# Outputs of three expert quads kept as DRAM rows and gathered in the fourth quad, in place of one-hot scatter products

## The chip, the cores and the metric

The kernel runs on one core of a Trainium2 chip. The metric is the device time of one execution in microseconds. The kernel before takes 929.15 us, the median of three runs (928.97 to 929.91).

## The reference, cut to what matters

Two trunk layers, each a mixer and then a mixture of 16 experts in 4 groups; a token goes to the best group and there to its best two experts. Layer 0 works on 512 tokens (256 latent, 256 context), layer 1 on the 256 latent ones. All in float32, width 1024, expert width 512.

```python
pg, g = lax.top_k(p_grp, 1)                       # group of the token
pe, ie = lax.top_k(jax.nn.softmax(logits_sel), 2)  # two experts in it
wts = pg * pe / jnp.sum(pe, axis=-1, keepdims=True)
eid = g * EXPERTS_PER_GROUP + ie
for e in range(N_EXPERTS):
    a = jax.nn.silu(h @ w_gate[e]) * (h @ w_up[e])
    y = y + gates[:, e:e + 1] * (a @ w_down[e])
x = x + g2 * y
```

So 1024 pairs (token, expert) in layer 0, each with one output row of 1024 numbers, and each token adds two such rows.

## The kernel before, in words

The change is in the experts of layer 0 (function `experts`, with `l == 0`). The 16 experts are taken in four "quads" of four. A quad has 384 slots, as three tiles of 128 (`nst = 3`): each expert has 64 slots in the first two tiles and 32 more in the third, and the third tile is worked on only in quads where some expert has more than 64 pairs. In the traced execution that is so in quads 1 and 2. Code that runs only then stands under `beyond(q)`, a branch on a register that every engine takes by itself.

A quad takes three phases of four weight chunks, 2 MB each: gate (`wg`, into PSUM banks `ga`), up (`wu`, into `ua`) and down (`wd`, into `da`). The down phase has two halves of 512 output columns, each of two chunks. Weights come by SyncE's DMA queue into a ring of five buffers and one more (`slot0`), so chunk n is fetched when TensorE has let go of chunk n - 6. PSUM has four `acc` banks, two `aux` and two `tmp`.

TensorE's input for a quad is `XT`, its tokens' rows, transposed. For quads 1 to 3, `slots(q)` builds a one-hot matrix `SS` (slot by token), `fetch` makes an index per slot out of it (`ii`, on VectorE, three buffers) and GpSimd gathers the rows from DRAM (`xg`, three buffers of 128 x 1024, an indirect DMA each; from quad 2 on a second one for the gates). `turn` transposes them, between the matmuls of the quad before.

What a quad puts out is added to the tokens by matmuls: `halves` splits a half of the output into two parts `oh` (ScalarE's cast) and `ol` (VectorE's difference), `combine` multiplies both by `SS` (128x512 matmuls, two for each 128 columns and tile), and `add` multiplies by the gate of the modulation and adds into `X` (`xl` latent, `xc` context, tokens along the free axis). The second half's `combine` of a quad is `pending` and runs behind the first gate chunk of the next quad. The last quad does the same with its last 512 columns cut in two.

The order on each engine is that of a list scheduler, except for instructions under `tc.keep_in_program_order`, which stay as written. Engines take their instructions in that order, so one that waits holds all behind it.

The code ahead of the experts that matters here: the routing (`Route.choose`, `Route.slots`, one chain on VectorE, shown under line 89, the wrapper that pins it) ends in `vec`, from which the `OH` one-hots (`one_hots`) of quad 0 are built; TensorE waits for these before it gathers quad 0's tokens by matmul (line 1036).

Of the kernel before, what the change touches and what calls it, by code (L numbers as in the profile page):

```python
# [12 lines left out]
F32 = mybir.dt.float32  # L13
# [22 lines left out]
HW = 0  # L36
EXTRA = 1
CAP = {0: 96, 1: 64}


PAR_BMOD, PAR_NG, PAR_WR, PAR_BR, PAR_PSC = 0, 96, 128, 448, 488
PAR_W = 492

CO_ID, CO_ONE, CO_TOK, CO_SLOT, CO_BEFORE, CO_BASE, CO_QUAD, CO_FIRST = 0, 128, 256, 768, 788, 804, 836, 840
CO_W = 844

MC_ROT, MC_MASK = 0, 512
MC_W = 768
# [8 lines left out]
def build(tc, ctx, a, cap=CAP):  # L57
# [7 lines left out]
    shd = dram.tile([1, 2 * D], F32, name="shd")  # L65
    h2d = dram.tile([T, D], F32, name="h2d")
    gd = dram.tile([T, 4], F32, name="gd")

    def phase(name, side="left"):
        return tc.tile_pool(name=name, bufs=1, side=side, reuse_waits="tile")  # L70
# [97 lines left out]


    def transpose(out, in_):  # L170
        PE.transpose(out, in_, ident)  # L171

    def keep_warm(n, bank=tmp):

# [141 lines left out]
    def drain(g):  # L316
        out = None
        for out in g:
            pass
        return out  # L320
# [433 lines left out]
    class Route:  # L754


        def __init__(self, l, nt, small, rt):
            self.l, self.nt, self.rt = l, nt, rt
            self.small, self.used = small.tile([P, 130 * nt], F32, name="small"), 0
            self.vec = small.tile([P, 4, nt], F32, name="vec")  # L760
            self.gov = small.tile([P, nt, 16], F32, name="gov")
            self.flag = small.tile([P, 1], I32, name="flag")
            self.plan = small.tile([P, 8], I32, name="plan")

        def new(self, *shape):
# [103 lines left out]
        def slots(self, rk):  # L869
            l, nt = self.l, self.nt  # L870
            V_ = pinned(V)
            r = rk[:, 0:nt * 16].rearrange("p (t c) -> p t c", t=nt)
            ov = self.ov = self.new(nt, 16)
            V_.tensor_scalar(ov, r, float(CAP[l]), None, op0=ALU.is_ge)
            t = self.rt.work[:, 0:48 * nt]
            t0 = t[:, 0:nt * 16].rearrange("p (t c) -> p t c", t=nt)
            V_.scalar_tensor_tensor(t0, ov, -1e6, self.base[:, None, :].to_broadcast([P, nt, 16]),
                                    op0=ALU.mult, op1=ALU.add)
            V_.tensor_tensor(t0, t0, r, op=ALU.add)
            m = t[:, nt * 16:nt * 48]  # L880
            V_.tensor_tensor(m.rearrange("p (i m) -> p i m", i=2), self.M.rearrange("p (i t) c -> p i (t c)", i=2),
                             t[:, None, 0:nt * 16].to_broadcast([P, 2, nt * 16]), op=ALU.mult)
            V_.tensor_reduce(self.vec[:, 0:2, :].rearrange("p i t -> p (i t)"),
                             m.rearrange("p (m c) -> p m c", c=16), axis=AX.X, op=ALU.add)

        def gates(self):
            nt, new, over = self.nt, self.new, self.over
# [156 lines left out]
                    V.tensor_scalar(XT[:, k, c0:c1], y[:, :W], sh[k], None, op0=ALU.add)  # L1044


    def experts(l, nt, h2, vec, gov, fv, place, more, XT, xpool, pool, where, last):
        n = nt * P
        nst = 3 if l == 0 else 2
        W = nst * P  # L1050
# [113 lines left out]
        if l == 0:  # L1164
            x8 = slot0[0].tile([P, 2048], F32, tag="x", name="x8")
            yg = itertools.cycle([x8[:, 1536:1792], x8[:, 1792:2048]])
        pending = []
        sq = []
        quad = [0]
        for q in range(4):  # L1170
# [4 lines left out]
            for ch in range(4):  # L1175
                w = ahead.pop(0) if ahead else weights(a["wg"][l, place[q], ch])
                drain(tiles([(ch * 2 + kk, XT[:, ch * 2 + kk, :], w[:, kk]) for kk in range(2)], KD - 1, ga,
                            ch % 2 == 0))
                if ch == 0:
                    while pending:  # L1180
                        pending.pop()()
                if ch == 1 and q == 2:
                    overflow(l, nt, h2, gov, fv, pool)
                if ch == 0 and q == 0:
                    rows(range(2))
                    if l == 0:
                        nSS, xg = slots(1)
                if ch == 1 and q == 0:
                    rows(range(2, 4))
                    SS, _ = slots(0, False)  # L1190
            sg = []
            for st in range(2):
                t = pool.tile([P, DE], F32, tag="sg", name="sg", bufs=3 - l)
# [5 lines left out]
            for ch in range(4):  # L1199
                w = weights(a["wu"][l, place[q], ch])  # L1200
                drain(tiles([(ch * 2 + kk, XT[:, ch * 2 + kk, :], w[:, kk]) for kk in range(2)], KD - 1, ua,
                            ch % 2 == 0))
            if l:
                gt = gates(q)
            elif q == 0:
                gts = gates(0), gates(1)
                gt = gts[0]
            turning = iter(())
            if q < 3:
                if l:  # L1210
# [11 lines left out]
            def turned(st):  # L1222
                tp = tmp()
                for f in range(4):
                    transpose(tp[:, f * P:(f + 1) * P], sg[st][:, f * P:(f + 1) * P])
                V.tensor_copy(aT[:, :, st * P:(st + 1) * P], tp.rearrange("p (f t) -> p f t", f=4))  # L1226

            for st in range(2):
                V.scalar_tensor_tensor(sg[st], ua[st], gt[:, st:st + 1], sg[st], op0=ALU.mult, op1=ALU.mult)  # L1229
                turned(st)  # L1230
            if nst == 3:
                sg.append(pool.tile([P, DE], F32, tag="sg", name="sg", bufs=3 - l))
                with beyond(q):
                    S.activation(sg[2], ga[2], AF.Silu)
                    V.scalar_tensor_tensor(sg[2], ua[2], gt[:, 2:3], sg[2], op0=ALU.mult, op1=ALU.mult)
# [12 lines left out]
            def halves(da, c0=0, c1=512, parts=None):  # L1248
                if parts is None:
                    parts = [pool.tile([P, nst, 512], F32R, tag=x, name=x, bufs=2 - l) for x in ("oh", "ol")]  # L1250

                def part(st):
                    oh, ol = [x[:, st, c0:c1] for x in parts]
                    S.copy(oh, da[st][:, c0:c1])  # L1254
                    V.tensor_tensor(ol, da[st][:, c0:c1], oh.bitcast(F32), op=ALU.subtract)  # L1255

                part(0)
                part(1)
                if nst == 3:
                    with beyond(q):  # L1260
                        part(2)
                return parts

            def combine(hf, parts, k0=0, k1=4, bank=acc, q=q, SS=SS):
                for kk in range(k0, k1, 2):
# [33 lines left out]
                    nc.scalar.dma_start(a["out"][:, k, :], X[0][:, k, :])  # L1299

            da = [[acc() if hf == 0 or i < nst - 2 else aux() for i in range(nst)] for hf in range(2)]
            if q < 3:
                p = []
                for hf in range(2):
                    for c in range(2):
# [43 lines left out]
    for l in range(L):  # L1349
# [21 lines left out]
        with phase(f"mix{l}", "right") as pool:  # L1371
# [40 lines left out]
            OH = one_hots(nt, W, names, ro.vec, keep, ("pT", "s512"), T, 4, F32 if l else F32R, pinned(V))  # L1412
            if l == 0:
                drain(ro.plans)
            next(filler, None)
            if l == 0:
                for tt in range(nt):
# [8 lines left out]
        with phase(f"xt{l}") as hp:  # L1426
# [23 lines left out]
            keep_stack.close()  # L1450
            with phase(f"ex{l}") as pool:
                where = itertools.cycle([ring] * 5 + ([spare] * EXTRA + early if l else slot0))
                nxt = experts(l, nt, None if l == 0 else h2, vec, gov, fv, place, more, XT, hp, pool, where, l == L - 1)
        rp_stack.close()
        slot_stack.close()

# [2 lines left out]
def constants():  # L1459
# [12 lines left out]
    co[:, CO_BASE + 16:CO_BASE + 32] = np.arange(16) * 64 + 1  # L1472
    co[:, CO_QUAD:CO_QUAD + 4] = np.arange(4)
    co[:, CO_FIRST:CO_FIRST + 4] = [-100, 1, 2, 3]

    mc = np.zeros((P, MC_W), f)
    mb = np.zeros((P, MB_PW), f)
# [101 lines left out]
```

## Time and profile before

| | |
|---|---|
| median of three runs | 929.15 us |
| the profiled execution | 929.26 us |
| its span, first to last instruction | 927.4 us |
| mean granted TensorE clock | 0.979 |
| TensorE busy (PE) | 865.7 us, 93% |
| VectorE (DVE), ScalarE (ACT), GpSimd (POOL) busy | 409.9, 265.9, 64.5 us |
| bytes moved by DMA | 287.14 MB, mean 310 GB/s |

The profiled execution is 1.86 us longer than its span, and 0.11 us above the median. In the rows, a timeline row gives start, length, engine, line, operation, output and input with their size, and in brackets the idle time of the engine ahead of it and what ended it. Layer 0's experts run from about 262 to 552 us: quad 0 to 326, quad 1 to 411, quad 2 to 495, and the last quad to 552; then comes layer 1.

### The profile page before, as it was taken

How to read it: one execution, taken by the hardware profiler on the slowest of the kernel's cores; microseconds unless marked ns; L12 is line 12 of the kernel's file. 1: busy time of each engine (PE TensorE's matmuls, PEld its weight loads, DVE VectorE, ACT ScalarE, POOL GpSimd, SP SyncE). 2: the span in 40 equal slices, each digit the busy share in tenths (PEclk: the TensorE clock that was granted, in tenths of full speed). 3: DMA queues.
4: the chain of work that ended last, by engine and by line, in shares of the span. 5: the costliest groups of instructions: out<-in, count | busy, mean ns of one | idle time of the engine just before them, and what ended most of it. 6: DMA issues, size and time to landing. Idle time of an engine off the chain costs nothing. (4 is left out here: it accounts for less than half of the span.)

```text
span 927.4 us, 13199 instructions
## 1 busy us (share of the span) xinstructions
PE 865.7 (93%) x5078; PEld 478.1 (52%) x5078; DVE 409.9 (44%) x1028; ACT 265.9 (29%) x579; POOL 64.5 (7%) x74
## 2 busy tenths in 40 slices
PE   3899999999589999999999989989999999979998
PEld 2588676776353332442344357756973444434435
DVE  1467677633975230332221148877555241222212
ACT  3344667424320100110011055466422011100101
POOL 1000000001410030012000020000000000000000
PEclk9999999999699999999999998999999999989999
DMA  9645753744979999759958953985978999999981
GB/s 359 277 177 207 290 214 137 281 182 160 357 269 429 426 370 423 306 211 363 426 211 334 382 216 117 412 357 199 366 304 313 430 424 428 428 410 427 428 288 47
DMA packets 33826, 287.14 MB, mean 310 GB/s; under 512 B 3533, under 2 KB 13389, under 8 KB 17105
## 3 DMA queue, kind: packets, MB, share of 16 engines
q1 hardware_dynamic: 29168, 276.94, 74.3%
q0 software_dynamic: 1696, 5.79, 1.6%
q10 hardware_dynamic: 2880, 3.35, 1.0%
q8 instruction: 49, 0.80, 0.3%
q14 instruction: 33, 0.26, 0.1%
HBM read 282.90 MB, written 3.16 MB: 308 GB/s over the span
## 5 line engine op out<-in xcount | busy, mean ns | idle before, releaser
L1136 PE MATMUL acc<-w,XT 128*64 128x512 f32 (+1 forms) x768 | 171.3, 604 | 9.1 <-PEq L950 5.5
L1136 PE MATMUL aux<-w,XT 128*64 128x512 f32 (+1 forms) x512 | 109.1, 593 | 0.7 <-PEq L1146 0.7
L1136 PEld LDWEIGHTS acc<-w,XT 128*64 128x64 f32 (+1 forms) x768 | 51.5, 134 | 108.0 <-issue 103.8
L1136 PEld LDWEIGHTS aux<-w,XT 128*64 128x64 f32 (+1 forms) x512 | 33.6, 130 | 66.1 <-issue 65.3
L1136 PE MATMUL acc<-w,x 128*64 128x512 f32 (+2 forms) x272 | 55.3, 575 | 2.9 <-PEq L1146 2.3
L192 PE MATMUL aux<-w,c 128*32 128x512 f32 x368 | 49.5, 657 | 0.0
L1229 DVE SCALAR_TENSOR_TENSOR sg<-aux,gt,sg 128x512 f32<-128x512 f32 x12 | 9.0, 750 | 82.1 <-PE aux L1136 81.4
L115 DVE TENSOR_TENSOR wl<-w,wh 128x768 fp32r<-128x768 f32 (+2 forms) x48 | 43.8, 955 | 3.1 <-ACT wh L115 2.7
L1255 DVE TENSOR_TENSOR ol<-acc,oh 128x512 fp32r<-128x512 f32 (+1 forms) x25 | 15.7, 627 | 57.2 <-ACT oh L1254 57.0
L137 PE MATMUL acc<-wh,hh 128*128 128x512 f32 x96 | 38.3, 399 | 2.2 <-ACT hh L300 2.2
L1254 ACT CAST oh<-acc 128x512 fp32r<-128x512 f32 (+1 forms) x25 | 13.4, 534 | 94.0 <-PE acc L1136 93.9
L115 ACT CAST wh<-w 128x768 fp32r<-128x768 f32 (+2 forms) x48 | 37.5, 831 | 7.9 <-DMA w<-w_out 3.8
L138 PE MATMUL acc<-wl,hh 128*128 128x512 f32 x96 | 37.9, 394 | 0.0
L139 PE MATMUL acc<-wh,hl 128*128 128x512 f32 x96 | 37.8, 393 | 0.0
L1194 ACT ACTIVATE sg<-acc 128x512 f32<-128x512 f32 x16 | 9.4, 597 | 87.0 <-PE acc L1136 87.0
L525 ACT ACTIVATE pr<-acc,soft 128x512 f32<-128x512 f32 (+1 forms) x48 | 29.4, 619 | 11.7 <-DVE soft L522 11.7
L1136 PEld LDWEIGHTS acc<-w,x 128*64 128x64 f32 (+1 forms) x272 | 15.6, 130 | 32.6 <-issue 31.6
L1136 PE MATMUL aux<-w,aT 128*64 128x512 f32 (+2 forms) x192 | 29.1, 453 | 0.0
L1136 PE MATMUL acc<-w,aT 128*64 128x512 f32 (+1 forms) x160 | 28.8, 511 | 0.2 <-DVE aT L1226 0.2
L574 PE MATMUL aux<-pT,vt 128*64 128x128 f32 x320 | 27.3, 281 | 0.4 <-ACT pT L549 0.2
L1102 ACT COPY XT<-tmp 128x512 f32<-128x512 f32 x6 | 3.5, 585 | 81.6 <-PE tmp L171 81.6
L1292 DVE SCALAR_TENSOR_TENSOR xl<-tmp,modT,xl 128x256 f32<-128x256 f32 x24 | 11.2, 481 | 33.2 <-PE tmp L1272 33.0
(329 smaller groups left out, 1581.7 us busy)
## 6 DMA issues: line engine op xcount, KB each, us to landing
w<-wg SPq DMA_DIRECT2D x32, 2048.0 KB, 13.1
w<-wu SPq DMA_DIRECT2D x32, 2048.0 KB, 11.5
w<-wd SPq DMA_DIRECT2D x29, 2048.0 KB, 12.0
w<-w_mod SPq DMA_DIRECT2D x23, 2048.0 KB, 12.6
w<-w_out SPq DMA_DIRECT2D x4, 2048.0 KB, 8.3
w<-wd SPq DMA_DIRECT2D x6, 1024.0 KB, 13.4
w<-w_qkv SPq DMA_DIRECT2D x3, 1536.0 KB, 8.3
w<-w_pf SPq DMA_DIRECT2D x2, 2048.0 KB, 7.9
```

The lines of the kernel that those rows point to most:

```text
L115: return S.copy(hi, x), eng.tensor_tensor(lo, x, hi.bitcast(F32), op=ALU.subtract)
L137: PE.matmul(out, lhs[0], rhs[0], start=start, stop=False, skip_group_check=True)
L138: PE.matmul(out, lhs[0], rhs[1], start=False, stop=False, skip_group_check=True)
L139: PE.matmul(out, lhs[1], rhs[0], start=False, stop=stop, skip_group_check=True)
L192: mm = PE.matmul(m[32 * j:32 * j + 32, :], sc2[:, k, :], w[:, kk, j * 512:(j + 1) * 512], start=(ch == chs[0] and kk == 0), stop=(ch == ch ...
L525: S.activation(pr[e], sp[e], AF.Exp, bias=nm[:, e:e + 1], scale=SCALE, accum_out=sums[:, e:e + 1])
L574: PE.matmul(o[e * 64:(e + 1) * 64, c * P:(c + 1) * P], vt[:, k0 + m, e * 64:(e + 1) * 64], pTs[e * nk + m], start=(m == 0), stop=(m == nk ...
L1136: PE.matmul(o, lh, r, start=(k == 0), stop=(k == last_k), skip_group_check=True)
L1194: S.activation(t, ga[st], AF.Silu)
L1254: S.copy(oh, da[st][:, c0:c1])
L1255: V.tensor_tensor(ol, da[st][:, c0:c1], oh.bitcast(F32), op=ALU.subtract)
L1292: V.scalar_tensor_tensor(x, y[:, s * N:(s + 1) * N], g, x, op0=ALU.mult, op1=ALU.add)
```

## The change

In layer 0 the outputs of the first three quads are no longer multiplied by `SS`. A new `store` copies each tile of a half from PSUM to SBUF (ScalarE the first and third tile, VectorE the second) and GpSimd's queue writes it, 128 rows of 512 numbers, to its place in a DRAM array `yd` of 1152 rows and one row of zeros. Without a third tile something else is written in its place. That is 18 writes of 256 KB.

A new `places`, nine operations on VectorE in the routing, makes for every token the two rows of `yd` that it adds (the row of zeros for a pair that isn't in the first three quads). `collect`, called after the third and the fourth chunk of the last quad's up phase, gathers these rows on GpSimd's queue, two indirect DMAs of 512 KB for each of four tiles of 128 tokens, adds the two on VectorE (pinned), transposes the sum on TensorE (32 transposes in all, pinned) and adds it into `X` with the modulation's gate. The last quad keeps its scatter products.

```diff
@@ class Route
+        def places(self, rk):
+            nt = self.nt
+            c16 = [co[:, CO_ROW + i * 16:CO_ROW + (i + 1) * 16] for i in range(2)]
+            r = rk[:, 0:nt * 16].rearrange("p (t c) -> p t c", t=nt)
...
+            V.tensor_tensor(b, self.base, c16[1], op=ALU.add)
+            V.tensor_scalar(t, r, 64.0, None, op0=ALU.is_ge)
+            V.tensor_tensor(t, t, c16[0][:, None, :].to_broadcast([P, nt, 16]), op=ALU.mult)
+            V.tensor_tensor(t, t, r, op=ALU.add)
+            V.scalar_tensor_tensor(t, self.ov, 1e6, t, op0=ALU.mult, op1=ALU.add)
+            V.tensor_tensor(t, t, b[:, None, :].to_broadcast([P, nt, 16]), op=ALU.add)
+            V.tensor_tensor(m.rearrange("p (i t) c -> p i (t c)", i=2), self.M.rearrange("p (i t) c -> p i (t c)", i=2),
+                            t.rearrange("p t c -> p (t c)")[:, None, :].to_broadcast([P, 2, nt * 16]), op=ALU.mult)
+            V.tensor_reduce(f, m, axis=AX.X, op=ALU.add)
+            V.tensor_scalar(self.rows, f, float(YD), None, op0=ALU.min)
@@ experts, ahead of the quads
+            z = pool.tile([P, D], F32, tag="xg", name="z", bufs=3)
+            G.memset(z[0:1, :], 0.0)
+            G.dma_start(yd[YD:YD + 1, :], z[0:1, :])
+        def collect(tts):
+            for tt in tts:
+                if tt in (1, 2):
+                    g = [pool.tile([P, nst, 512], F32, tag=("oh", "ol")[tt - 1], name="yr", bufs=2)[:, 0:2, :]
+                         .rearrange("p a b -> p (a b)") for _ in range(2)]
+                else:
+                    g = [pool.tile([P, D], F32, tag="xg", name="yr", bufs=3) for _ in range(2)]
+                for i in range(2):
+                    G.indirect_dma_start(out=g[i], out_offset=None, in_=yd[:, :],
+                                         in_offset=bass.IndirectOffsetOnAxis(ap=places[:, i * nt + tt:i * nt + tt + 1], axis=0))
+                tc.keep_in_program_order(V.tensor_tensor(g[0], g[0], g[1], op=ALU.add))
+                for i in range(2):
+                    t = tmp()
+                    for c in range(4):
+                        tc.keep_in_program_order(
+                            transpose(t[:, c * P:(c + 1) * P], g[0][:, (i * 4 + c) * P:(i * 4 + c + 1) * P]))
+                    for c in range(4):
+                        k = i * 4 + c
+                        x = X[tt // 2][:, k, tt % 2 * P:tt % 2 * P + P]
+                        V.scalar_tensor_tensor(x, t[:, c * P:(c + 1) * P], modT[l][:, 40 + k, tt // 2:tt // 2 + 1], x,
+                                               op0=ALU.mult, op1=ALU.add)
@@ experts, in a quad
-                    SS, _ = slots(0, False)
+                    SS = None if l == 0 else slots(0, False)[0]
...
+                if l == 0 and q == 3 and ch > 1:
+                    collect(range(2 * ch - 4, 2 * ch - 2))
...
-                gts = gates(0), gates(1)
-                gt = gts[0]
+                gt = gates(0)
...
+            def store(da, hf):
+                ys = pool.tile([P, nst, 512], F32, tag=("oh", "ol")[hf], name="ys", bufs=2)
+                def put(st, y):
+                    r0 = q * 384 + st * P
+                    G.dma_start(yd[r0:r0 + P, hf * 512:(hf + 1) * 512], y)
+                for st in range(2):
+                    (V.tensor_copy if st else S.copy)(ys[:, st, :], da[st])
+                    put(st, ys[:, st, :])
+                with beyond(q) as there:
+                    S.copy(ys[:, 2, :], da[2])
+                    put(2, ys[:, 2, :])
+                with there.Else():
+                    put(2, ys[:, 0, :])
...
-            if q < 3:
+            if l == 0 and q < 3:
+                for hf in range(2):
+                    for c in range(2):
+                        down(da[hf], 2 * c, weights(wd(l, place[q], 2 * hf + c)))
+                    store(da[hf], hf)
+            elif q < 3:
@@ layer 0, routing
                 drain(ro.plans)
+                ro.places(rk)
```

How this moves instructions is seen at three places. The first is TensorE in the last quad, from the last matmuls of the third up chunk to the transposes of `sg` ahead of the down phase; before:

```order
L1136 MATMUL aux<-w,XT 64x512 x2
L1146 COMPARE_AND_BRANCH
L1136 MATMUL aux<-w,XT 32x512 x16
L1146 UNCONDITIONAL_BRANCH x2
L1233 COMPARE_AND_BRANCH
L1233 UNCONDITIONAL_BRANCH x2
L1136 MATMUL acc<-w,XT 64x512 x2
L1136 MATMUL aux<-w,XT 64x512 x2
L1136 MATMUL acc<-w,XT 64x512 x2
L1136 MATMUL aux<-w,XT 64x512 x2
L171 MATMUL tmp<-co,sg 128x128 x8
```

and now, where `yr` is a gathered sum of rows, the end of the third chunk:

```order
L1161 MATMUL aux<-w,XT 64x512 x2
L173 MATMUL tmp<-co,yr 128x128 x8
L1171 COMPARE_AND_BRANCH
L1161 MATMUL aux<-w,XT 32x512 x16
L1171 UNCONDITIONAL_BRANCH x2
```

with, a few rows on, the fourth chunk:

```order
L1161 MATMUL acc<-w,XT 64x512 x2
L1161 MATMUL aux<-w,XT 64x512
L173 MATMUL tmp<-co,yr 128x128 x8
L1161 MATMUL aux<-w,XT 64x512
L1161 MATMUL acc<-w,XT 64x512 x2
L1161 MATMUL aux<-w,XT 64x512 x2
L173 MATMUL tmp<-co,yr 128x128 x16
L173 MATMUL tmp<-co,sg 128x128 x8
```

The eight transposes of the first token tile stand right behind the third chunk, those of the second inside the fourth chunk, and those of the third and fourth behind it, ahead of everything of the down phase.

The second place is GpSimd from quad 2's second half on (the stores of quad 2's first half stand just ahead of these rows); before, none of these DMAs stands there.

```order
L1324 DMA yd<-ys 128x512 [waits DMASW2_49,Activation_49]
L1329 UNCONDITIONAL_BRANCH
L1324 DMA yd<-ys 128x512 [waits DMASW3_49]
L1324 DMA yd<-ys 128x512 [waits DMASW4_49,DVE_49]
L1204 DMA yr<-yd,rows 128x1024 [waits DMASW3_49,DMASW4_49,DMASW2_49,DMASW5_49,DMASW1_49,DMASW7_49,DMASW0_49,PE_49]
L1204 DMA yr<-yd,rows 128x1024 [waits DMASW6_49,PE_49]
L1204 DMA yr<-yd,rows 128x1024 x2
L869 TENSOR_LOAD plan
L1171 COMPARE_AND_BRANCH
L1171 UNCONDITIONAL_BRANCH x2
L1204 DMA yr<-yd,rows 128x1024
L1204 DMA yr<-yd,rows 128x1024 [waits Activation_49]
```

The first gather waits for the landing of the stores (the DMASW semaphores are those of GpSimd's queue).

The third place is VectorE in quad 0's down phase, between its first and second half. Before, `ol` is the split of the output:

```order
L1104 COPY XT<-tmp 128x4x128 [waits PE_49]
L1146 COMPARE_AND_BRANCH
L1146 UNCONDITIONAL_BRANCH x2
L1260 COMPARE_AND_BRANCH
L1255 TENSOR_TENSOR ol<-acc,oh 128x512 [waits DVE_49,Activation_49]
L1260 UNCONDITIONAL_BRANCH
L1260 UNCONDITIONAL_BRANCH [waits DVE_49]
L1104 COPY XT<-tmp 128x4x128 [waits PE_49]
L1255 TENSOR_TENSOR ol<-acc,oh 128x512 [waits DVE_49,Activation_49]
L1104 COPY XT<-tmp 128x4x128 [waits PE_49]
```

and now, where `ii` is an index of the fetches for the last quad:

```order
L1129 COPY XT<-tmp 128x4x128 [waits PE_49]
L1329 COMPARE_AND_BRANCH
L1329 UNCONDITIONAL_BRANCH x2
L1109 TENSOR_SCALAR ii<-ix 128x1 [waits DMASW7_49,DMASW2_49]
L1327 COPY ys<-acc 128x512 [waits DMAHW2_49,PE_49]
L1107 SCALAR_TENSOR_TENSOR sk,ix<-SS,co 128x512 [waits DVE_49]
L1129 COPY XT<-tmp 128x4x128 [waits PE_49]
L1109 TENSOR_SCALAR ii<-ix 128x1 [waits DMASW5_49,DMASW0_49]
L1109 TENSOR_SCALAR ii<-ix 128x1 [waits DMASW7_49,DMASW1_49,DVE_49]
```

The scheduler has pulled the index work for the last quad up into quad 0. Each `ii` takes the buffer of one of quad 2's indices and waits for that fetch to land, and the copies of quad 0's output out of PSUM (`ys<-acc`, and a `ys<-aux` after these rows) stand behind it.

## Rows read from the trace of the kernel before

**Rows 1.** The page, busy time of TensorE.
```profile
PE 865.7 (93%) x5078; PEld 478.1 (52%) x5078; DVE 409.9 (44%) x1028; ACT 265.9 (29%) x579; POOL 64.5 (7%) x74
```
**Rows 2.** Busy time by stretch: the four quads (the last in two), then layer 1's start.
```profile
core 0: us, PE busy (x) PEld busy (x) DVE busy (x) ACT busy (x) POOL busy (x), PEclk, DMA share, GB/s
262.00:326.00 64.00, 60.37 (x280) 24.94 (x277) 33.50 (x87) 9.49 (x16) 4.67 (x5) 1.00 0.93 382
326.00:411.00 85.00, 83.37 (x477) 32.27 (x478) 23.23 (x50) 9.60 (x18) 11.03 (x13) 1.00 0.85 342
411.00:495.00 84.00, 81.79 (x472) 31.23 (x470) 22.25 (x47) 8.65 (x16) 9.35 (x11) 1.00 0.81 323
495.00:525.00 30.00, 29.02 (x132) 10.49 (x129) 2.28 (x5) 1.67 (x3) 0.73 (x1) 1.00 0.88 346
525.00:552.00 27.00, 24.53 (x136) 12.72 (x134) 9.13 (x19) 9.42 (x22) 5.24 (x6) 1.00 0.80 295
552.00:564.00 12.00, 9.04 (x42) 5.75 (x40) 8.53 (x18) 5.64 (x12) 1.43 (x2) 0.58 0.00 0
```
**Rows 3.** SyncE's queue, waits in quads: line, waited for, us, times, longest.
```profile
SPq L108 <- PE acc L1136: 109.1, 19, 11.6
```
**Rows 4.** The same view by stretch, 298 to 326 us alone.
```profile
298.00:326.00 28.00, 25.98 (x115) 10.79 (x113) 9.02 (x17) 4.46 (x8) 1.46 (x2) 1.00 1.01 427
```
**Rows 5.** Scatter products of quads 0 to 2 alone, line 1272, by eleven stretches.
```profile
314.00:318.70 4.70, 3.16 (x11) 1.84 (x11) 1.00 1.00 425
...
497.00:499.00 2.00, 0.96 (x3) 0.48 (x3) 1.00 0.04 16
sum 40.40, PE 33.89 PEld 22.70; mean PE 3.08 PEld 2.06
```
**Rows 6.** Timeline of TensorE: transposes of fetched rows, last quad's start, its down phase.
```profile
374.30 1.06 PE L171 MATMUL tmp<-co,xg 128*128 128x128 f32 x8 [0.83 <-PE tmp L171]
...
494.27 3.65 PE L1136 MATMUL acc<-w,XT 128*64 128x512 f32 x16
...
526.50 3.65 PE L1136 MATMUL acc<-w,x 128*64 128x512 f32 x16 [0.30 <-PEq L1244]
...
551.87 0.40 PE L1272 MATMUL acc<-SS,ol 128*128 128x512 f32 x1
```
**Rows 7.** Timeline of VectorE: the routing; quad 1's first tile leaves `xg`.
```profile
245.58 0.28 DVE L89 TENSOR_TENSOR rw<-small,rw 128x128 f32<-128x128 f32 x1
...
309.99 0.69 DVE L1104 COPY XT<-tmp 128x512 f32<-128x512 f32 x1
```
**Rows 8.** TensorE's waits, 240 to 262 us.
```profile
PE acc L1036 <- DVE OH L89: 5.9, 1, 5.9
```
**Rows 9.** GpSimd's fetches of rows, 334 to 450 us: issue to landing.
```profile
DMA to landing us min/median/max: 10.7/15.8/18.5
```
**Rows 10.** Timeline of ScalarE: third and last copies out of quad 2's output banks.
```profile
472.43 0.59 ACT L1254 CAST oh<-acc 128x512 fp32r<-128x512 f32 x1 [0.27 <-PE acc L1136]
...
489.31 0.59 ACT L1254 CAST oh<-aux 128x512 fp32r<-128x512 f32 x1 [0.27 <-PE aux L1136]
```
**Rows 11.** DMA queues, 336 to 361 us: packets, MB, share; issues, us to landing.
```profile
DMA packets 1126, 10.35 MB, mean 414 GB/s; under 512 B 207, under 2 KB 207, under 8 KB 591
## 3 DMA queue, kind: packets, MB, share of 16 engines
q1 hardware_dynamic: 597, 8.75, 83.0%
q0 software_dynamic: 528, 1.58, 16.3%
...
xg<-h2d,ii POOLq DMA_INDIRECT x3, 13.3
```
**Rows 12.** The same view, 422 to 447 us.
```profile
xg<-h2d,ii POOLq DMA_INDIRECT x3, 18.5
```
**Rows 13.** The same view, 237 to 254 us: a 1 MB write to DRAM.
```profile
h2d<-xt ACTq DMA_DIRECT2D x2, 1024.0 KB, 16.1
```
**Rows 14.** Timeline of TensorE, layer 1: a chunk behind an idle stretch.
```profile
818.21 6.33 PE L1136 MATMUL acc<-w,XT 128*64 128x512 f32 x16 [4.80 <-PEq L950]
```
**Rows 15.** Busy time in that stretch, with its granted clock.
```profile
818.00:825.00 7.00, 6.79 (x18) 2.40 (x19) 3.15 (x9) 0.00 (x0) 0.00 (x0) 0.60 1.00 417
```

More of the change, by code (lines that the diff above doesn't have):

```diff
@@ L38 @@
 CAP = {0: 96, 1: 64}
+YD = 3 * 384
 PAR_BMOD, PAR_NG, PAR_WR, PAR_BR, PAR_PSC = 0, 96, 128, 448, 488
 PAR_W = 492
-CO_ID, CO_ONE, CO_TOK, CO_SLOT, CO_BEFORE, CO_BASE, CO_QUAD, CO_FIRST = 0, 128, 256, 768, 788, 804, 836, 840
-CO_W = 844
+CO_ID, CO_ONE, CO_TOK, CO_SLOT, CO_BEFORE, CO_BASE, CO_QUAD, CO_FIRST, CO_ROW = 0, 128, 256, 768, 788, 804, 836, 840, 844
+CO_W = 876
 MC_ROT, MC_MASK = 0, 512
@@ L67, in build @@
     gd = dram.tile([T, 4], F32, name="gd")
+    yd = dram.tile([YD + 1, D], F32, name="yd")
     def phase(name, side="left"):
@@ L170, in transpose @@
     def transpose(out, in_):
-        PE.transpose(out, in_, ident)
+        return PE.transpose(out, in_, ident)
     def keep_warm(n, bank=tmp):
@@ L762, in __init__ @@
             self.flag = small.tile([P, 1], I32, name="flag")
+            self.rows = small.tile([P, 2 * nt], I32, name="rows") if l == 0 else None
             self.plan = small.tile([P, 8], I32, name="plan")
@@ L884, in slots @@
                              m.rearrange("p (m c) -> p m c", c=16), axis=AX.X, op=ALU.add)
+        def places(self, rk):
+            nt = self.nt
+            c16 = [co[:, CO_ROW + i * 16:CO_ROW + (i + 1) * 16] for i in range(2)]
+            r = rk[:, 0:nt * 16].rearrange("p (t c) -> p t c", t=nt)
+            w = self.rt.work[:, 324:]
+            b = w[:, 0:16]
+            t = w[:, 16:80].rearrange("p (t c) -> p t c", t=nt)
+            m = w[:, 80:208].rearrange("p (m c) -> p m c", c=16)
+            f = w[:, 208:208 + 2 * nt]
+            V.tensor_tensor(b, self.base, c16[1], op=ALU.add)
[8 more added lines that the diff above has]
+            V.tensor_scalar(self.rows, f, float(YD), None, op0=ALU.min)
         def gates(self):
@@ L1044, in gather, with experts @@
                     V.tensor_scalar(XT[:, k, c0:c1], y[:, :W], sh[k], None, op0=ALU.add)
-    def experts(l, nt, h2, vec, gov, fv, place, more, XT, xpool, pool, where, last):
+    def experts(l, nt, h2, vec, gov, fv, place, more, places, XT, xpool, pool, where, last):
         n = nt * P
@@ L1230, in experts @@
                 turned(st)
+            if l == 0 and q == 0:
+                gts = gt, gates(1)
             if nst == 3:
@@ L1452, in build @@
                 where = itertools.cycle([ring] * 5 + ([spare] * EXTRA + early if l else slot0))
-                nxt = experts(l, nt, None if l == 0 else h2, vec, gov, fv, place, more, XT, hp, pool, where, l == L - 1)
+                nxt = experts(l, nt, None if l == 0 else h2, vec, gov, fv, place, more, ro.rows, XT, hp, pool, where, l == L - 1)
         rp_stack.close()
@@ L1474, in constants @@
     co[:, CO_FIRST:CO_FIRST + 4] = [-100, 1, 2, 3]
+    j = np.arange(16) % 4
+    co[:, CO_ROW:CO_ROW + 16] = 192 - 32 * j
+    co[:, CO_ROW + 16:CO_ROW + 32] = -32 * j - 1
     mc = np.zeros((P, MC_W), f)
```

## The prediction

> **What bounds the kernel now.** I read the page's busy times first, then a table of the four quads by stretch, then the waits of SyncE's queue, then timelines at the places where the change cuts in. TensorE is busy 93% of the span [rows 1], and in the quads 60.4 of 64, 83.4 of 85, 81.8 of 84 and 53.6 of 57 us [rows 2]. So what TensorE loses in instructions there is time, as long as the weights keep up. They nearly don't: the DMA share is 0.80 to 0.93 in the quads, and in 298 to 326 us it is 1.01 at 427 GB/s, which I take as all that the engines move [rows 2, 4]. SyncE spends long waits on TensorE's release of buffers (19 of them, 109 us, for one kind of bank alone), so in the rest the ring, not the wire, holds the weights back [rows 3]. From rows 2 the wire is busy 59.5 + 72.3 + 68.0 + 26.4 + 21.6 = 247.8 of these 290 us (length times share, in turn); 42 us are free. Behind 552 us nothing moves [rows 2], so a shift of the last quad's end passes whole into the end of the run.
>
> **The change part by part.**
>
> *Scatter products, removed.* The 128 products of line 1272 for quads 0 to 2 cost 33.9 us of TensorE [rows 5], in stretches where it hardly idles: **-33.9**. Of it 0.96 us lie behind the last quad's first chunk, 32.9 ahead of its start at 494.27 [rows 5, 6]. With them go the additions into `X`, which were off TensorE's path.
>
> *Places, added.* Nine operations on VectorE stand in the chain that TensorE waits on for 5.9 us [rows 8], ahead of the last one-hots. The 128x128 one took 0.28 us [rows 7]; nine of these would be 2.5, none on the path 0. Two are that large, the others 64 columns or less, and some fall into gaps of the scheduler: **+1.3**, bounds 0 to 2.5.
>
> *Index work pulled into quad 0, moved.* `ii` for the last quad now waits for quad 2's fetches to land, and behind it in VectorE's queue stand the copies that empty quad 0's output banks. Quad 2's first fetch can start when its buffer's last reader is through, about 310 us [rows 7], and lands 10.7 to 18.5 us later [rows 9], at 320.7 to 328.5. With 9.2 us less of products (three of the eleven stretches, the first 3.16 us [rows 5]) and 1.3 more, quad 1 starts at about 318. It has four `acc` banks and needs three, one of them the bank behind the first `ii`. That makes a stall of 2.7 to 10.5 us, or none if the scheduler's order leaves the bank free. A first fetch has a queue of its own ahead of the other two, so I take the quick end: **+3.0**, bounds 0 to 12 (a late third fetch included).
>
> *Stores, added.* 18 DMAs of 256 KB, 4.7 MB. They go beside work, in free wire time. The only one that is waited for is the last, by the first gather. Quad 2's copies out of PSUM end at 472 to 489 [rows 10]; less what has been removed by then, 18.3 and 24.5 us, the stores are issued from about 454 to 465. Nearest rows: 1.58 MB of fetches share the wire with weights and take 16.3% of it, some 69 GB/s [rows 11]; a write of 1 MB landed after 16.1 us [rows 13]. Six stores, 1.57 MB, at 50 to 69 GB/s need 23 to 31 us from 454: landed between 477 and 485, some five later if they are slower still. I take 488.
>
> *Gathers, adds and transposes, added.* 32 transposes at 1.06/8 us [rows 6]: **+4.2** on TensorE. The wait in front of them is the large unknown. The last quad starts at 494.27 - 32.9 + 1.3 + 3.0 = 465.7, its gate and up phases take 3.67 us a chunk (3.65 in [rows 6]), so TensorE stands in front of the first transposes at 491.4, as the gathers have only just been issued. Two gathers of 512 KB and an addition: at the low end of [rows 9] the first tile is there at 501. The bytes bound the last: from 466 until then about seven and a half chunks of 2.1 MB, half of the stores and 4.2 MB of gathers, 20.7 MB, at 427 GB/s [rows 4] 48 us, so 513 to 514. That holds because weights can't run further than the ring while TensorE stands, and then the gathers have the wire. With the last transposes and the turning of `sg`, the down phase starts at 516. Without any wait it would start at 465.7 + (526.50 - 494.27 - 0.96) + 4.2 = 501.2. So the wait is **+14.8**, bounds 0 (all landed in time) and 36 (each gather at the slow end of rows 9, below).
>
> *The clock.* A chunk that followed 4.8 us of idle took 6.33 us at a granted clock of 0.60, the 1.2 GHz level, against 3.65 at full clock [rows 6, 14, 15]: **+2.7** for one such chunk behind the wait, bounds 0 to 5.4.
>
> *At nothing.* Copies to SBUF instead of two-part splits (ScalarE and VectorE do less); the zero row (long ahead); the branch's other side; the gates of quad 1, moved behind `sg`. These lie beside TensorE's matmuls. If the copies were late, the next quad's gate phase would wait for the bank; that is the third term.
>
> Sum: -33.9 + 1.3 + 3.0 + 4.2 + 14.8 + 2.7 = -7.9. Made against the profiled execution, 929.26 us (0.1 above the median), this is 921.4; I say 921.
>
> Two rules weighed. The DMA engines in [rows 11] moved 528 packets for fetches and 597 for weights, near one for one, while the bytes stood 1.58 to 8.75. The Trainium skill, "DMA: Bandwidth & Descriptors", section "Queues, rings and completion order", says that each DMA engine goes round its queues packet by packet; the trace agrees. By that rule small packets keep a small share as long as weights run, which speaks against this change, whose rows are small; it is how I read the 69 GB/s, and the sum stands as it is. The same page, section "Anatomy of one DMA — SWDGE (gpsimd) path", gives a fit of about 2.0 us and bytes over 436 GB/s for a DMA of GpSimd's; an estimate from it is 3.2 us for 512 KB. The trace of before disagrees while weights run, 10.7 us at the least [rows 9]. By that fit the wait would be gone; it is the first rival's case.
>
> **The rivals.**
>
> *No wait.* Stores land in time and gathers slip in beside the weights. Then the sum is -33.9 + 1.3 + 3.0 + 4.2 = -25.4: 904. For it: 42 us of free wire in the quads [rows 2] against 8.9 MB more, 21 us at 427 GB/s. Against it: bytes alone allow no more than 42 - 21 = 21 us of gain (908), and the gathers can't be issued before quad 2's last store, 26 us ahead of the place where they are used. Time 904 to 909.
>
> *Slow gathers, the change loses.* The gathers keep the small share throughout. Three fetches took 13.3 and 18.5 us in the median [rows 11, 12], so 4.4 to 6.2 us apiece when several run together; eight from 488 last until 523 to 538. Every microsecond that the last one lands behind 513 is one more of TensorE standing; the gain is gone from 521 on. In the middle, 531: 921 + 18 = 939. For it: the share in rows 11 and the long ring of weights. Against it: TensorE stands still then, the ring fills (six chunks, some 12.6 MB, 29 us) and weights stop.
>
> *The gain is swallowed.* The same 513, but the stall in quad 1 is 10 us and is not made up, or the last weights of the last quad, pushed behind the gathers, come late for the down phase by as much: 929.
>
> *It doesn't do what it says.* A token's two rows might not be spread as assumed, but gathers have a fixed size; nothing here depends on the routing except the third tile, the same as before. No chance of its own.
>
> **How the numbers follow.** My forecast (905 to 927, mostly 915 to 926) gets 0.56, no wait 0.12, the swallowed gain 0.12, slow gathers 0.20. About 0.2%, 1.9 us, is what a measurement tells from no change. Faster: 0.56 + 0.12 = 0.68; within 0.2%: 0.12; slower: 0.20. Range for 8 in 10: below 905 lies half of the no-wait case (0.06), above 937 a little over half of the slow one (0.12), so 905 to 937. The forecast's own range is 912 to 927.
>
> **What would show it.** In the stretch of the last quad: TensorE's wait for VectorE's sum in front of the first `yr` transposes, 8 to 11 us, and again in front of the later ones, 15 us in all, then a chunk at about 0.6 clock; the down phase starting at 516 and the layer ending near 544 (25.8 us later [rows 6], and the clock). Gathers landing at 500 to 514, the first at least 10 us after its issue. Quad 1's start at 318 to 321, with a VectorE wait on a DMA ahead of it. Products of line 1272 only in the last quad, none of the 33.9 us. I'm wrong if no `yr` transposes wait, if the last gather lands behind 521, or if the stall in quad 1 is above 8 us.

## The result, and the profile after

The changed kernel takes 924.06 us, the median of five runs (921.91 to 927.35), against 928.97 for the kernel before (928.38 to 929.91): a ratio of 0.9948, 95% interval 0.9924 to 0.9972. A later job gave 924.25 against 929.11, 0.9945 (0.9928 to 0.9962). So 4.9 us are gained of the 33.9 of removed products. Forecast were 921, a range of 905 to 937, and faster with a chance of 0.68. The profiled execution took 922.93 us with a span of 921.1; its 6.3 us less of span are what the rows below add up to.

The stretches that answer to [rows 2] (the columns are the same; quads 0, 1 and 2, then the last quad up to the end of the third up chunk, from there to the down phase, and the down phase):

```profile
262.00:320.60 58.60, 52.04 (x244) 21.64 (x244) 31.73 (x78) 7.17 (x11) 10.28 (x10) 0.94 0.96 383
320.60:394.80 74.20, 70.04 (x426) 22.97 (x422) 11.66 (x26) 5.03 (x9) 10.39 (x15) 1.00 1.01 427
394.80:465.20 70.40, 68.92 (x418) 22.74 (x420) 7.57 (x11) 4.54 (x9) 3.60 (x5) 1.00 0.93 376
465.20:495.00 29.80, 25.06 (x114) 10.44 (x110) 1.11 (x7) 1.68 (x3) 8.28 (x10) 1.00 1.01 427
495.00:518.60 23.60, 13.10 (x56) 7.09 (x56) 15.58 (x40) 0.00 (x0) 0.94 (x1) 0.72 1.04 404
518.60:547.10 28.50, 26.42 (x128) 12.70 (x128) 11.53 (x20) 12.12 (x26) 5.72 (x6) 0.93 0.40 159
```

The wire, 0.80 to 0.93 busy in the quads before, is now full through quad 1 and through the last quad until its down phase. TensorE works 13.1 of 23.6 us in the fifth stretch, at a granted clock of 0.72 (1 is the 2.4 GHz level). TensorE's timeline shows why (it answers to [rows 6]):

```profile
245.78 3.25 PE L1061 MATMUL acc<-OH,h2h 128*128 128x256 f32 x12 [4.50 <-DVE OH L91]
...
258.37 3.65 PE L1161 MATMUL acc<-w,XT 128*64 128x512 f32 x16 [2.39 <-DVEq L1523]
...
298.20 1.97 PE L173 MATMUL tmp<-co,sg 128*128 128x128 f32 x8 [3.97 <-DVE sg L1281]
300.48 3.68 PE L1161 MATMUL acc<-w,x 128*64 128x512 f32 x8 [0.30 <-PEq L1298]
...
465.25 3.60 PE L1161 MATMUL acc<-w,XT 128*64 128x512 f32 x16
...
500.82 1.97 PE L173 MATMUL tmp<-co,yr 128*128 128x128 f32 x8 [10.10 <-DVE yr L1206]
503.25 1.98 PE L1161 MATMUL acc<-w,XT 128*64 128x512 f32 x4 [0.45 <-PEq L1171]
...
514.32 1.09 PE L173 MATMUL tmp<-co,yr 128*128 128x128 f32 x8 [2.95 <-DVE yr L1206]
516.19 2.15 PE L173 MATMUL tmp<-co,sg 128*128 128x128 f32 x8 [0.78 <-DVE xc L1215]
518.64 3.65 PE L1161 MATMUL acc<-w,x 128*64 128x512 f32 x6 [0.30 <-PEq L1298]
...
528.39 0.59 PE L1161 MATMUL aux<-w,x 128*64 128x256 f32 x2
...
546.73 0.40 PE L1343 MATMUL acc<-SS,ol 128*128 128x512 f32 x1
```

TensorE stands 10.1 us in front of the first token tile's transposes and 2.95 in front of the last one's; eight transposes behind the long wait take 1.97 us in place of 1.06, and the first matmuls of the down phase (six on record) 3.65 us, at a granted clock of 0.51, the 1.2 GHz level (the columns are those of [rows 2]):

```profile
518.60:522.70 4.10, 3.65 (x6) 0.78 (x6) 0.47 (x1) 0.00 (x0) 0.00 (x0) 0.51 0.47 196
```

Three moments of the timeline before that [rows 6] do not have: the start of quad 0's first gate chunk, the start of its down phase, and in the last quad's down phase the first matmul into `aux`:

```profile
261.20 3.65 PE L1136 MATMUL acc<-w,XT 128*64 128x512 f32 x16 [2.04 <-ACTq L1446]
...
298.54 1.94 PE L1136 MATMUL acc<-w,x 128*64 128x512 f32 x8 [0.30 <-PEq L1244]
...
534.53 0.60 PE L1136 MATMUL aux<-w,x 128*64 128x256 f32 x4
```

The span of each kernel, cut at the same moments:

| stretch, us | before | after | difference |
|---|---|---|---|
| start of the span to quad 0's first gate chunk | 261.20 | 258.37 | -2.8 |
| from there to quad 0's down phase | 37.3 | 42.1 | +4.8 |
| from there to the last quad | 195.7 | 164.8 | -31.0 |
| the last quad's gate and up phases | 32.2 | 53.4 | +21.2 |
| its down phase | 25.4 | 28.1 | +2.7 |
| from the start of its last product to the end | 375.5 | 374.4 | -1.2 |

VectorE's and GpSimd's waits, 260 to 560 us (what, on what, us, times, longest):

```profile
DVE ii L1109 <- DMA xg<-h2d,ii: 38.2, 5, 11.6
```

```profile
POOL yr L1204 <- DMA yd<-ys: 15.0, 1, 15.0
POOL yr L1204 <- DVE yr L1206: 9.9, 1, 9.9
```

The chain of the last quad can be followed by issues and landings: the last store was issued at 467.1 us and landed at 481.6, GpSimd having waited 15.0 us for it; the first two gathers, issued at 482.6 and 483.9, landed at 494.0 and 499.5, and the addition ran at 499.54:

```profile
499.54 1.22 DVE L1206 TENSOR_TENSOR yr<-yr 128x1024 f32<-128x1024 f32 x1 [32.94 <-DMA yr<-yd,rows]
...
509.00 1.22 DVE L1206 TENSOR_TENSOR yr<-yr 128x1024 f32<-128x1024 f32 x1
510.13 0.75 DVE L1281 SCALAR_TENSOR_TENSOR sg<-acc,gt,sg 128x512 f32<-128x512 f32 x1
510.97 2.16 DVE L1215 SCALAR_TENSOR_TENSOR xc<-tmp,modT,xc 128x128 f32<-128x128 f32 x8
513.04 1.22 DVE L1206 TENSOR_TENSOR yr<-yr 128x1024 f32<-128x1024 f32 x1
```

From the second tile on nothing waits for a DMA any more. VectorE comes to the next addition after 4.7 us and, from the third tile to the fourth, after 4.04 (addition, a piece of the last quad's own work, eight updates of X), with no idle time in that last round; TensorE's later transposes follow that pace.

### The profile page after: what moved, and what is told of

Same layout as the page of the kernel before. It is cut to its first block, busy times and chain, and to the rows that moved or that the text cites. A ratio compares the mean times of both kernels' runs of the same rounds, so it can differ in the third digit from the quotient of the medians.

```text
span 921.1 us, 12893 instructions
## 1 busy us (share of the span) xinstructions
PE 843.2 (92%) x4982; PEld 464.9 (50%) x4982; DVE 399.1 (43%) x1024; ACT 255.1 (28%) x558; POOL 74.3 (8%) x87
## 5 line engine op out<-in xcount | busy, mean ns | idle before, releaser
L1161 PE MATMUL aux<-w,XT 128*64 128x512 f32 (+1 forms) x512 | 111.1, 594 | 0.6 <-PEq L1171 0.6
L1161 PEld LDWEIGHTS acc<-w,XT 128*64 128x64 f32 (+1 forms) x768 | 53.4, 133 | 109.4 <-issue 102.5
L1161 PE MATMUL acc<-w,x 128*64 128x512 f32 (+2 forms) x272 | 58.8, 597 | 1.4 <-PEq L1171 0.6
L141 PE MATMUL acc<-wh,hl 128*128 128x512 f32 x96 | 38.2, 398 | 0.0
L1161 PEld LDWEIGHTS acc<-w,x 128*64 128x64 f32 (+1 forms) x272 | 17.5, 134 | 33.7 <-issue 32.7
L1308 ACT CAST oh<-acc 128x512 fp32r<-128x512 f32 (+1 forms) x14 | 6.9, 493 | 93.7 <-PE acc L1161 89.1
L1161 PE MATMUL aux<-w,x 128*32 128x512 f32 (+2 forms) x144 | 25.8, 546 | 0.5 <-PEq L1171 0.5
L263 POOL TENSOR_TENSOR part<-part,sq 128x512 f32<-128x512 f32 (+1 forms) x12 | 14.2, 1180 | 145.8 <-ACT sq L259 142.7
## 6 DMA issues: line engine op xcount, KB each, us to landing
w<-wg SPq DMA_DIRECT2D x32, 2048.0 KB, 13.1
```

Of the source, the lines that this page charges most:

```text
L141: PE.matmul(out, lhs[1], rhs[0], start=False, stop=stop, skip_group_check=True)
L263: (V, G)[k % 2].tensor_tensor(p[:, :n], p[:, :n], sq[:, :n], op=ALU.add)
L1161: PE.matmul(o, lh, r, start=(k == 0), stop=(k == last_k), skip_group_check=True)
```

## The experiments

**Sums in the down phase.** Gathers issued as before, the rest of `collect` behind the two first down chunks:

```diff
-                tc.keep_in_program_order(V.tensor_tensor(g[0], g[0], g[1], op=ALU.add))
+                rowsums.append((tt, g))
+        def finish(m):
+            for tt, g in [rowsums.pop(0) for _ in range(m)]:
+                tc.keep_in_program_order(V.tensor_tensor(g[0], g[0], g[1], op=ALU.add))
...
                             down(da[hf], 2 * c, weights(wd(l, place[q], 2 * hf + c)))
+                            if rowsums:
+                                finish(2)
```

> The changed kernel, with the gathers issued where they were, but the additions, transposes and updates of X taken into the last quad's down phase: two token tiles behind its first down chunk, two behind its second. Theory (TensorE stands because the pinned transposes are put in front of the down phase, while the first down chunk is already in SBUF at 500.7 us): the down phase starts at about 501 in place of 518.6, the waits for the sums shrink from 14.5 us to 3 to 6, the whole ends 10 to 14 us earlier than the changed kernel, near 912. Rival (the wire sets the end: gathers and weights share it, and the down chunks come late instead): the wait goes over to the weights and the time stays within 3 us of 924.

911.45 us (909.18 to 915.26), ratio to before 0.9821 (0.9799 to 0.9843), 12.6 us under the changed kernel. TensorE's timeline of this kernel:

```profile
498.06 3.65 PE L1161 MATMUL acc<-w,x 128*64 128x512 f32 x16 [0.30 <-PEq L1305]
501.84 1.06 PE L173 MATMUL tmp<-co,yr 128*128 128x128 f32 x8
...
505.85 1.09 PE L173 MATMUL tmp<-co,yr 128*128 128x128 f32 x8 [0.90 <-DVE yr L1213]
...
511.22 0.65 PE L1161 MATMUL acc<-w,x 128*64 128x256 f32 x4 [1.56 <-DMA w<-wd]
```

The down phase starts at 498.1, the first transposes find their sum ready, and the wire shows itself in 1.56 us of waiting for a weight chunk, no more. The position of the sums and transposes was the price, as the theory has it.

**No collect.**

```diff
-                if l == 0 and q == 3 and ch > 1:
-                    collect(range(2 * ch - 4, 2 * ch - 2))
```

> The changed kernel without collect: the three quads' outputs are stored but never gathered, so their contribution to X is left out. Theory (the second half of the change gives back some 22 us: 4.2 of transposes, 14.5 of waits, about 5 of low clock): 924 - 22 = 902, with quad 3 of layer 0 starting at 465 as in the changed kernel. Rival (the 4.7 MB of stores and the full wire are what holds the last quad): the last quad still waits, for weights, and the time is 912 or more.

897.84 us (897.70 to 899.81), ratio 0.9675 (0.9661 to 0.9689). Storing in place of the products, with what the places and the index work give and cost, is worth 31.4 us; gathering gives 26.2 back, four more than I had expected. The last quad starts at 464.4, its down phase at 495.8, without a wait for weights: the rival falls. The sums are wrong in this run, but it takes 374.8 us behind layer 0's last product, the changed kernel 374.4; so layer 1 does not disturb the comparison.

**Nine index buffers.**

```diff
-            ii = pool.tile([P, 1], I32, tag="ii", name="ii", bufs=3)
+            ii = pool.tile([P, 1], I32, tag="ii", name="ii", bufs=9)
```

> The changed kernel with nine index buffers in place of three, so that no index operation waits for a fetch to land. The waits of VectorE on fetches (38 us in five waits) go, and with them TensorE's 4.0 us in front of the transposes of sg in quad 0 and the low clock behind it. Theory (TensorE's time passes through to quad 3, whose stores and gathers come earlier by as much): 3 to 6 us faster than the changed kernel, 918 to 921. Rival (the wire, full from 300 to 440 us, sets when quad 3's gathers land): no change, 923 to 925.

919.27 us (916.66 to 923.02), ratio 0.9896 (0.9874 to 0.9919), 4.8 us under the changed kernel. The waits of `ii` are gone from VectorE's list, and quad 0's transposes start without one:

```profile
293.79 0.66 PE L173 MATMUL tmp<-co,sg 128*128 128x128 f32 x4
294.65 0.66 PE L173 MATMUL tmp<-co,sg 128*128 128x128 f32 x4 [0.20 <-DVE sg L1281]
```

In the traces the last quad starts 4.8 us earlier than the changed kernel's (460.42 against 465.25) and its down phase 3.8 (514.85 against 518.64). So most of the gain goes through, although the changed kernel's wire is full through quad 1; the first theory holds.

**Places alone**, in the kernel before:

```diff
                 drain(ro.plans)
+                ro.places(rk)
```

> The kernel before, with nothing of the change but the nine operations of places in the routing, whose result is not used. Theory from the changed kernel's trace (the scheduler, with nine more operations to place, puts four splits of h2 behind the one-hots instead of among the chain that leads to them): 1.4 to 2.8 us faster than before, 926 to 927.6. Rival (my prediction's term: nine operations on the chain cost 1.3 us, and the earlier start in the changed kernel's profile has another cause): 930.3. Third: within 0.5 us of before.

927.15 us (924.92 to 929.72), ratio 0.9981 (0.9970 to 0.9992). Nine operations added on the way to the one-hots, and the kernel is 2.1 us faster. VectorE's timeline in this kernel shows the cause; before, four splits `h2l` of 0.68 us stood between 244.24 and 247.18, ahead of the first one-hot at 247.62. The first view is before's, the second this kernel's:

```profile
247.62 0.62 DVE L89 SCALAR_TENSOR_TENSOR OH<-names,vec,sj 128x384 fp32r<-128x384 f32 x1
```

```profile
244.96 0.41 DVE L90 TENSOR_SCALAR sj<-names,vec 128x384 f32<-128x384 f32 x1
245.29 0.21 DVE L903 SCALAR_TENSOR_TENSOR rw<-small,rw 128x64 f32<-128x64 f32 x1
245.42 0.61 DVE L90 SCALAR_TENSOR_TENSOR OH<-names,vec,sj 128x384 fp32r<-128x384 f32 x1
...
249.97 0.68 DVE L116 TENSOR_TENSOR h2l<-xt,h2h 128x512 fp32r<-128x512 f32 x1
```

Now one split is left ahead of the one-hots, and short operations of `places` fill the places of the others.

**Both edits together** (sums in the down phase, nine index buffers).

> Both edits that helped in one kernel: sums and transposes in the down phase (911.45 alone) and nine index buffers (919.27 alone, 4.8 under the changed kernel). Theory (two separate stalls of TensorE, quad 0 and quad 3, that add up): 906 to 908. Rival (with the first stall gone the last quad runs into the wire, and its weights or gathers come late by as much): 910 to 912.

906.83 us (905.98 to 908.08), ratio 0.9760 (0.9748 to 0.9773): the two gains add up (17.2 us under the changed kernel, 12.6 and 4.8 alone), and this version beats both kernels.

**All of collect behind the fourth up chunk.**

```diff
-                if l == 0 and q == 3 and ch > 1:
-                    collect(range(2 * ch - 4, 2 * ch - 2))
+                if l == 0 and q == 3 and ch == 3:
+                    collect(range(4))
```

> The changed kernel with all four token tiles behind the fourth up chunk in place of two behind the third. Theory (the last gather's landing, 510 us, sets the start of the down phase, wherever TensorE stands before): within 2.5 us of the changed kernel, 922 to 926. Rival (standing in the middle of the up phase is itself the cost, since the fourth chunk's 3.6 us could have run in the wait): 918 to 921.

923.86 us (922.12 to 925.91), ratio 0.9940 (0.9927 to 0.9953), no change against the changed kernel. The first wait is 6.2 us in place of 10.1, but then each tile waits 2.5 to 3.0 us for VectorE, 14.2 in all. The down phase starts at 520.3. What sets it is not the last landing (510.4), as I had written, but the four tiles from 500 us on, one after another, 4.5 us each: VectorE adds (1.2 us), waits 1.2 for TensorE's transposes, runs the eight updates (2.2) and only then comes to the next addition. The time came out as expected, for another reason.

**Gathers from an old array.**

```diff
-            V.tensor_scalar(self.rows, f, float(YD), None, op0=ALU.min)
+            V.tensor_scalar(self.rows, f, float(T - 1), None, op0=ALU.min)
...
-                    G.indirect_dma_start(out=g[i], out_offset=None, in_=yd[:, :],
+                    G.indirect_dma_start(out=g[i], out_offset=None, in_=h2d[:, :],
```

> The changed kernel with its eight gathers reading the array of token rows h2d, written long before, in place of yd, so that they don't wait for the stores; the stores stay, the sums are of other rows. Theory (the wait begins with the landing of quad 2's stores, 14.6 us after the last issue, and the gathers that follow it): most gathers land before TensorE is at the end of the third up chunk, its waits go from 14.5 to under 4 us and the time is 905 to 911. Rival (the gathers' own share of the wire is what is waited for, not the stores): waits of 10 us or more remain and the time is 918 or more.

The whole took 4119 us, since with other sums layer 1 sends its tokens over the overflow path; only layer 0 is read. It settles less than it should. TensorE's waits were 16.3 us, which is the rival's sign; the first two tiles' transposes waited 0.0 and 0.81, as the theory has it, but the third 13.0:

```profile
492.06 1.09 PE L173 MATMUL tmp<-co,yr 128*128 128x128 f32 x8
...
496.35 1.09 PE L173 MATMUL tmp<-co,yr 128*128 128x128 f32 x8 [0.81 <-DVE yr L1206]
...
513.14 1.97 PE L173 MATMUL tmp<-co,yr 128*128 128x128 f32 x8 [12.98 <-DVE yr L1206]
```

Two of the tiles use the buffers out of which quad 2 is stored, so their gathers still waited for these stores (41.6 us of GpSimd's waits), and the run does not tell the theory from its rival.

**Two quads as rows, quad 2 by products.**

```diff
-YD = 3 * 384
+YD = 2 * 384
...
-            if l == 0 and q < 3:
+            if l == 0 and q < 2:
```

> The changed kernel with only the first two quads as DRAM rows; quad 2 keeps its 48 scatter products, its pairs read the row of zeros. Six stores fewer, and the gathers need only stores that landed long before the last quad. Theory (the chain from quad 2's last copy over its stores' landing to the gathers is what TensorE waits for): the 48 products cost 48 x 0.265 = 12.7 us, waits of 14.5 and some 4 of low clock go, the time is 914 to 920. Rival (gathers beside weights are slow wherever they stand, and the buffers of quad 2's splits free late): waits of 8 us or more remain and the time is 925 or more.

930.41 us (928.76 to 932.29), ratio 1.0015 (1.0004 to 1.0026). The waits fell to 4.0 us, as expected, and the last quad starts 12.3 us later, as expected; the time is nevertheless 10 us above my range. The transposes stand at 503.72, 508.01, 512.05 and 516.09, again 4.0 to 4.3 us apart: with the first rows long there, the pace of the tiles is left, the start of the down phase at low clock too, and it begins at 520.4. So in these traces giving up quad 2's rows costs layer 0 1.9 us more than it saves (its last product starts at 548.66, the changed kernel's at 546.73). Another 5 us were lost in layer 1, where the chunk from 815.55 us on took until 825.74, 10.2 us, with a break of 2.2 us in it, and the changed kernel's in the same place 5.1. Why stays open.

**Small matmuls before the transposes.** First as one block ahead of each of the two calls of `collect` (72 and 20 matmuls), then in front of each tile; the edit of the second run:

```diff
                 tc.keep_in_program_order(V.tensor_tensor(g[0], g[0], g[1], op=ALU.add))
+                keep_warm((72, 0, 4, 20)[tt])
...
+                if tt == 3:
+                    keep_warm(5)
```

> The changed kernel with 72 and 20 small matmuls, about 9 and 2.5 us, in front of the pinned transposes, so that TensorE is busy while it waits. Theory (after the wait TensorE runs at its lower clock: 2.7 us in the down phase, one or two in the fourth up chunk): 2 to 4 us faster than the changed kernel, 920 to 922. Rival (the landings set the pace and the clock costs nothing): 923 to 925, or later by what the matmuls run over.

> The changed kernel with small matmuls right in front of each token tile's transposes (72, 4 and 20, and 5 ahead of those of sg), so that TensorE is busy in all of its waits up to the down phase. Theory (the tail from the down phase's start to the last product is 28.5 us in the changed kernel and 25.8 before because of the lower clock): the tail is 25.8 again, the chunks of the down phase take 3.65 us and the time is 2 to 4 us under the changed kernel's in the same job. Rival (it isn't the clock; the tail waits for weights): the tail stays at 28 and the time doesn't move.

The first gave 922.14 us (921.30 to 924.54), ratio 0.9927 (0.9914 to 0.9941), whose interval overlaps the changed kernel's, between the two expectations; its second block had run before the waits that it was to fill. It shows one thing all the same. The transposes and the fourth up chunk ran at full clock; they began 0.5 us later than in the changed kernel (501.31), and the down phase 0.2 earlier (518.44), still at low clock. So low clock on these pieces had cost 0.7 us at most:

```profile
500.00:514.00 14.00, 9.86 (x60) 5.72 (x60) 12.40 (x30) 0.00 (x0) 0.94 (x1) 1.00 1.06 400
```

The second gave 920.70 (918.88 to 923.39), ratio 0.9903 (0.9886 to 0.9920), 3.5 us under the changed kernel in the same job, and the down phase begins at full clock:

```profile
521.24 1.90 PE L1161 MATMUL acc<-w,x 128*64 128x512 f32 x6 [0.39 <-DVE x L1281]
...
529.24 0.59 PE L1161 MATMUL aux<-w,x 128*64 128x256 f32 x2
...
547.23 0.40 PE L1346 MATMUL acc<-SS,ol 128*128 128x512 f32 x1
```

The tail is 26.0 us from 521.24, against 28.1 in the changed kernel and 25.4 before. To the first matmul into `aux` it takes 8.00 us, as before (8.03), against 9.75 in the changed kernel: that 1.7 us is the low clock, in the first group of matmuls (1.90 us here, 3.65 there). Of the 3.5 us the tail shows 2.1; the rest is not located.

> The changed kernel once more, unchanged, as the mark for the other two on the same chip: 922 to 926.

It gave 924.25 us (922.92 to 925.57).

## Why the prediction was right

Its main line is what the traces show: most of what the removed products give (31.0 us up to the last quad) goes again in the last quad (21.2 in its gate and up phases), as a wait for the gathers in front of the transposes, and as a start of the down phase at low clock. Of line 1272's products nothing is left in quads 0 to 2, and from quad 0's down phase to the last quad 31.0 us are gone, 32.9 forecast. The down phase was to begin at 516 and began at 518.6.

Two agreements on the way are luck. The last quad was to start at 465.7 and starts at 465.25, since three errors cancel by the table: the places were put 4.1 us too dear, the index work 1.8 too cheap, and the products' gain 1.9 too large. The first transposes were to start at 501 and start at 500.82: the stores landed at 481.6 in place of 488, but from there to the first tile's sum it took 19 us in place of 13. (The 18.3 and 24.5 us that the prediction takes off for the stores' issue should be 17.3 and 23.5: 21.6 and 27.8 us of products by then, less 1.3 and 3.0. Nothing hangs on that microsecond.)

Four things in it were off. *Places* were to cost 1.3 us and gave 2.1 (their own run; 2.8 in the changed kernel's trace); I had looked at what is added to the chain and not at what the scheduler takes out of it, though the order was there to be read. *The index work* was to cost 3.0 us in front of quad 1. The wait that I had named was there: VectorE stood 11.65 us for the fetch, with the copy of quad 0's output behind it. But quad 1 started without a stall. 4.0 us plus low clock were lost in quad 0's up phase, where the index operations for quad 2 wait for quad 1's fetches (280.36 and 292.59) ahead of the scaling of `sg`:

```profile
280.36 0.15 DVE L1109 TENSOR_SCALAR ii<-ix 128x1 int32<-128x1 f32 x1 [4.82 <-DMA xg<-h2d,ii]
...
292.59 0.15 DVE L1109 TENSOR_SCALAR ii<-ix 128x1 int32<-128x1 f32 x1 [1.12 <-DMA xg<-h2d,ii]
...
320.98 0.15 DVE L1109 TENSOR_SCALAR ii<-ix 128x1 int32<-128x1 f32 x1 [11.65 <-DMA xg<-h2d,ii]
```

```profile
320.63 22.23 PE L1161 MATMUL acc<-w,XT 128*64 128x512 f32 x132
```

I had counted only the index operations for the last quad. With nine buffers quad 0's down phase starts at 295.61 in place of 300.48, which is the whole gain of 4.8; the other 32 of the 38.2 us of waits cost TensorE nothing.

*The last wait* had the right size (14.8 forecast; 10.10 + 0.23 + 2.95 + 0.78 = 14.1 measured) for half a wrong reason. I bound it by bytes, 20.7 MB at the full wire. The wire was full, but the last gather, issued only when the first addition had freed its buffer at 501, landed at 510.1, and VectorE came to it at 513.04: the round of VectorE's addition, TensorE's transposes and VectorE's updates, which I gave nothing, sets the pace behind the first sum. From that addition to the down phase it took 5.6 us, where 2 to 3 had been allowed behind the last landing, which covers the 2.6 us by which the down phase came late.

*The clock* was to cost 2.7 us for a whole chunk of the down phase. The tail is 2.7 us longer, but by the second run with small matmuls only 1.7 of it is the low clock, which lasted for the first group of matmuls and not for a chunk; the other 1.0 stands behind it at full clock, and its cause stays open. That the sum is 2.7 again is luck. Low clock also fell on the fourth up chunk and the first transposes, which I didn't count; by the first run with small matmuls this cost 0.7 us at most.

The Trainium skill's fit in "DMA: Bandwidth & Descriptors", section "Anatomy of one DMA — SWDGE (gpsimd) path" (2.0 us and bytes over 436 GB/s), which stood behind the rival of no wait, makes 3.2 us an estimate for a gather; the eight took 9.1 to 18.3 us. In the run with the old array the first, with the wire partly free (a DMA share of 0.39 from 447.8 to 452.4 us), took 4.6.

## What to carry to other kernels

Ask of a pinned instruction on the busiest engine what it will stand in front of: the same gathers with their transposes a phase later were worth 12.6 us, more than the change itself. Work that a scheduler may pull forward brings its buffers' waits with it into an engine that takes its work in order; more buffers for a tile of 512 bytes gave 4.8 us. Where a long wait is removed, price the round of all engines in the chain behind it per tile, not only the engine that waits.

## What the runs showed of the hardware

Gathers' share of the wire depends on what they share it with. Beside weight chunks in large packets they had 16.3% [rows 11]; in the last quad, where half of the weights come as chunks of 1 KB rows, they had twice that (482 to 512 us; packets, MB, share):

```profile
q1 hardware_dynamic: 2692, 8.22, 67.8%
q0 software_dynamic: 1152, 4.19, 34.2%
```

Weights moved 3.1 KB a packet there (8.22 MB in 2692), 14.7 before. That fits turns by packet, and two shorter stretches show it better: the packets of the two queues go nearly one for one, as in [rows 11], while the gathers' share goes from 20.9% to 78.4%. From 491 to 497 us the weights still come in large packets, from 501 to 507 in those of 1 KB:

```profile
q1 hardware_dynamic: 143, 2.08, 81.0%
q0 software_dynamic: 141, 0.51, 20.9%
```

```profile
q0 software_dynamic: 531, 1.93, 78.4%
q1 hardware_dynamic: 527, 0.54, 25.3%
```

That may be why the gathers were through at 510 us where I had 513 to 514. The prediction counts on the weights to stop; they did not, but in packets of 1 KB they took a quarter of the wire.
